# A two-layer block in emulated fp32 on one core: the feed-forwards' first products for 16 of 22 column pairs by Strassen's seven products

## The chip, the core and the metric

The kernel runs on one core of one Trainium2 chip. A core has five engines with instruction queues of their own: TensorE (PE) multiplies matrices and writes to PSUM; VectorE (DVE), ScalarE (ACT) and GpSimd (POOL) work on tiles in SBUF and, except POOL here, read PSUM; SyncE (SP) issues the loads. Each engine runs its queue in order and waits at an instruction until what it needs is there. The metric is the device time of one execution in microseconds (us); the time of a kernel is the median of its runs.

## The reference

The input is x of 512 tokens by 1024 features, and two blocks are applied to it, with four gated feed-forwards among their parts:

```python
def swiglu_ffn(x, w_in, w_out):
    gate, up = jnp.split(x @ w_in, 2, axis=-1)
    return (jax.nn.silu(gate) * up) @ w_out

# first block
x = x + 0.5 * rms_norm(swiglu_ffn(rms_norm(x, norm_pre[l, 0]), ffn1_w_in[l], ffn1_w_out[l]), norm_post[l, 0])
x = x + rms_norm(token_mixer(rms_norm(x, norm_pre[l, 1]), ...), norm_post[l, 1])
x = x + 0.5 * rms_norm(swiglu_ffn(rms_norm(x, norm_pre[l, 2]), ffn2_w_in[l], ffn2_w_out[l]), norm_post[l, 2])
# second block
h = h + 0.5 * swiglu(rms_norm_2(h, ffn1_norm[i]), ffn1_w_in[i], ffn1_w_out[i])
h = h + merged @ w_out[i]                      # two kinds of attention and a gate
h = h + 0.5 * swiglu(rms_norm_2(h, ffn2_norm[i]), ffn2_w_in[i], ffn2_w_out[i])
h = h + sigmoid(rms_norm_2(h, ple_norm[i]) @ w_ple_gate[i]) * (p[i] @ w_ple_proj[i])
```

`w_in` is 1024 x 5632 (2816 gate columns, then 2816 up columns), `w_out` 2816 x 1024, everything in fp32. The change concerns `x @ w_in` of the four feed-forwards, which the kernel calls f1 and f2 (first block), f3 and f4 (second block).

## The kernel before

Activations lie with features on the partitions: x is 8 tiles of 128 features by 512 tokens. An fp32 product is emulated: each operand is split into a high part in TensorE's fast fp32 format and the low rest, and `mm3` (L258 to L261) sums three matmuls, high x high, high x low and low x high. A weight block goes through `wpiece` (L243 to L248): SP loads 128 columns of 8 k-tiles (a raw tile of 128 x 1024, three buffers), ScalarE writes the high part (L247), VectorE subtracts it from the raw tile and writes the low part (L248). Activations are split in the same way (`split`, L309 to L311). `lin` (L274 on) makes one output tile: 8 k-tiles times three matmuls of 512 columns into one PSUM bank.

In `ffn` the norm is applied late. The parts `us` hold x times the norm's gain; the sum of squares (ScalarE squares, POOL adds, L376) gives a factor for each token, which TensorE spreads over the partitions (L357) and VectorE copies to R (L395). Of the 22 pairs m, each 128 gate columns and the same 128 up columns, `lin` makes two banks; VectorE multiplies both by R on the way out of PSUM (L465, L466), ScalarE applies Silu, VectorE multiplies the two (L468), and the result is split at once into hi and lo (L310, L311), the operands of the second product. For f1, f2 and f3 `lin_ahead` computes pairs 0 and 1 in halves of 256 tokens while the phase before finishes; f4 has no such start. `late_constants`, rows that later phases need, is called at m = 2 of f1. `out_post` makes the second product (tiles f1o0, f1o1, ...: 22 k-tiles each, in three weight pieces) and the last of its tiles in halves of 256 tokens; then it applies the second norm and prepares the input of the next phase.

The order of the instructions is the work of a scheduler that goes by the program's order, the priorities from it and buffers that come free; parts of the mixers have a table of their own. So instructions of neighbouring pairs stand interleaved on an engine: in the trace TensorE runs a pair's 48 matmuls without a gap while VectorE splits weights two pairs ahead.

## Time and profile before

| | |
|---|---|
| runs | 2243.27, 2245.18, 2248.12 us; median 2245.18 |
| profiled execution | 2246.1 us, of which the span of the trace is 2244.3 |
| busy share of TensorE, VectorE, ScalarE, GpSimd | 99%, 51%, 39%, 6% |
| matmuls | 10922 |
| first products of f1, f2, f3, f4 (stretches of the span) | 219.98, 219.55, 219.10, 240.70 us |

The span is the time from the first to the last instruction in the trace. Busy shares are means over the span; matmuls overlap, so TensorE's share does not say how near to its peak it is. A tile's name in a row leaves out numbers: `f_12h_h` is the high part of activation 12 of a feed-forward, `f1o_p` an output bank of f1's second product. In brackets behind a row stands the idle time before it and what ended it.

### The profile page before, as it was taken

Reading aid. Unit: us, or ns where it says so; the run is one execution under the profiler, and the core shown is the slowest. Engines: PE = TensorE matmul, PEld = TensorE weight load, DVE = VectorE, ACT = ScalarE, POOL = GpSimd, SP = SyncE. Lnnn points to the kernel's source line nnn. Section 1 sums busy time; section 2 is a strip of 40 time slices with the busy share of each in tenths; the row PEclk is TensorE's granted clock in tenths of the full one; section 3 lists DMA queues with packets and bytes.
Section 4 is the critical chain, followed back from the end, with each engine's and each line's share of the span. In section 5 each row is a group of like instructions: output and inputs, shape, how many; then the busy total and the mean of one; then the engine's idle time right before and its main releaser. Section 6 shows DMA issues by size and latency. Waiting matters only on the chain.

```text
span 2244.3 us, 27350 instructions
## 1 busy us (share of the span) xinstructions
PE 2218.9 (99%) x10922; PEld 1844.9 (82%) x10922; DVE 1151.8 (51%) x1913; ACT 881.6 (39%) x1348; POOL 126.3 (6%) x168
## 2 busy tenths in 40 slices
PE   8999999999999999999999999999999999999999
PEld 7888888888788888889888888887877788888887
DVE  5644423878647544324644432487754554444334
ACT  4323323556545323223433222477654443323222
POOL 4000001100112000001000000000000010000000
PEclk9999999999989999999999999999999999999999
...
GB/s 152 94 96 102 88 100 94 85 66 77 38 47 85 94 102 96 90 100 83 97 100 94 92 96 101 97 75 51 63 80 29 84 108 99 94 95 96 97 108 66
DMA packets 364835, 197.20 MB, mean 88 GB/s; under 512 B 10007, under 2 KB 356516, under 8 KB 364708
## 3 DMA queue, kind: packets, MB, share of 16 engines
...
q14 instruction: 41, 0.34, 0.0%
q0 software_dynamic: 608, 0.09, 0.0%
...
## 4 chain that ended last, share of the span: by engine, by line
PE 97%; DVE 1%; ACT 1%; DMA 0%; issue 0%; SPq 0%; DVEq 0%; ACTq 0%
PE f1o_p L259 2%; PE f2o_p L260 2%; PE f1o_p L260 2%; PE f2o_p L259 2%; PE f2o_p L261 2%; PE f1o_p L261 2%; PE f4o_p L260 2%; PE f4o_p L259 2%; PE f3o_p L259 2%; PE f3o_p L260 2%; PE f3o_p L261 2%; PE f4o_p L261 2%; PE gt_p L259 1%; PE gt_p L260 1%; PE gt_p L261 1%; PE f_p L260 1%
## 5 line engine op out<-in xcount | busy, mean ns | idle before, releaser
L248 DVE TENSOR_TENSOR f1o_l<-f1o_r,f1o_h 128x1024 fp32r<-128x1024 f32 (+1 forms) x24 | 27.3, 1136 | 76.6 <-ACT f1o_h L247 76.6
L248 DVE TENSOR_TENSOR f2o_l<-f2o_r,f2o_h 128x1024 fp32r<-128x1024 f32 (+1 forms) x24 | 27.3, 1136 | 76.6 <-ACT f2o_h L247 76.6
L247 ACT ACTIVATE f1o_h<-f1o_r 128x1024 fp32r<-128x1024 f32 (+1 forms) x24 | 23.8, 990 | 85.7 <-PE f1o_p L260 73.0
L247 ACT ACTIVATE f2o_h<-f2o_r 128x1024 fp32r<-128x1024 f32 (+1 forms) x24 | 23.8, 990 | 85.7 <-PE f2o_p L260 73.0
L247 ACT ACTIVATE f4o_h<-f4o_r 128x1024 fp32r<-128x1024 f32 (+1 forms) x24 | 23.8, 990 | 85.3 <-PE f4o_p L260 53.2
L247 ACT ACTIVATE f3o_h<-f3o_r 128x1024 fp32r<-128x1024 f32 (+1 forms) x24 | 23.8, 990 | 85.3 <-PE f3o_p L260 53.2
L248 DVE TENSOR_TENSOR f3o_l<-f3o_r,f3o_h 128x1024 fp32r<-128x1024 f32 (+1 forms) x24 | 27.2, 1135 | 54.0 <-ACT f3o_h L247 54.0
L248 DVE TENSOR_TENSOR f4o_l<-f4o_r,f4o_h 128x1024 fp32r<-128x1024 f32 (+1 forms) x24 | 27.2, 1135 | 52.9 <-ACT f4o_h L247 52.9
L84 ACT ACT_TABLE_LOAD x36 | 46.2, 1283 | 1.4 <-PEq L1348 0.8
L376 POOL TENSOR_TENSOR f_acc<-f_acc,f_sq 128x256 f32<-128x256 f32 (+1 forms) x42 | 39.0, 929 | 127.5 <-ACT f_sq L375 110.0
L376 POOL TENSOR_TENSOR m_acc<-m_acc,m_sq 128x256 f32<-128x256 f32 (+1 forms) x18 | 20.0, 1114 | 349.0 <-ACT m_sq L375 349.0
L376 POOL TENSOR_TENSOR pl_acc<-pl_acc,pl_sq 128x512 f32<-128x512 f32 x6 | 10.3, 1710 | 340.7 <-ACT pl_sq L375 340.7
L261 PE MATMUL m1o_p<-mix_h,m1o_l 128*128 128x256 f32 (+1 forms) x88 | 29.4, 336 | 0.0
L260 PE MATMUL m1o_p<-mix_l,m1o_h 128*128 128x256 f32 (+1 forms) x88 | 29.4, 336 | 0.0
L259 PE MATMUL m1o_p<-mix_h,m1o_h 128*128 128x256 f32 (+1 forms) x88 | 28.7, 337 | 0.0
L376 POOL TENSOR_TENSOR f2p_acc<-f2p_acc,f2p_sq 128x512 f32<-128x512 f32 x6 | 7.7, 1287 | 323.2 <-ACT f2p_sq L375 323.2
L376 POOL TENSOR_TENSOR f1p_acc<-f1p_acc,f1p_sq 128x512 f32<-128x512 f32 x6 | 7.7, 1288 | 321.5 <-ACT f1p_sq L375 321.5
L259 PE MATMUL wo_p<-mg_h,wo_h 128*128 128x512 f32 x64 | 24.7, 389 | 0.0
L260 PE MATMUL wo_p<-mg_l,wo_h 128*128 128x512 f32 x64 | 24.7, 389 | 0.0
L261 PE MATMUL wo_p<-mg_h,wo_l 128*128 128x512 f32 x64 | 24.7, 389 | 0.0
L94 ACT ACTIVATE l<-l 128x384 f32<-128x384 f32 (+1 forms) x48 | 24.0, 558 | 0.7 <-DVE l L951 0.6
L247 ACT ACTIVATE pg_h<-pg_r 128x1024 fp32r<-128x1024 f32 x8 | 8.5, 1061 | 39.9 <-PE pg L498 12.7
...
## 6 DMA issues: line engine op xcount, KB each, us to landing
...
```

Of the source, the lines that this page charges most:

```text
L84: ld = S.preload_act_table_set(name).ins
L94: i = S.activation(out, in_, func, **kw).ins
L247: S.activation(hi, raw, AF.Copy)
L248: V.tensor_tensor(lo, raw, hi.bitcast(F32), ALU.subtract)
L259: M.matmul(o, w[0], u[0], start=first, stop=False)
L260: M.matmul(o, w[0], u[1], start=False, stop=False)
L261: issued["last"] = M.matmul(o, w[1], u[0], start=False, stop=last).ins.name
L376: G.tensor_tensor(acc[:, sl], acc[:, sl], q[:, sl], ALU.add)
```

## The change

Pairs 6 to 21 of each feed-forward are computed by Strassen's scheme in Winograd's form. The 1024 features fall into two halves of four k-tiles, the 512 tokens into two halves of 256, and gate and up columns are the two halves of the third dimension. Seven products of four k-tiles and 256 tokens (named by their input forms b11, b21, n1, t3, t2, b22, t4) replace eight. Pairs 0 to 5 stay as they were (`direct`).

- `strassen_input`: VectorE writes the normalised input un = x * gain * R (8 times 128 x 512); sums and differences of its quarters are made in place, and 28 forms of 128 x 256 are split into high and low parts (ScalarE and VectorE, 28 operations each).
- `strassen_pair`: two raw tiles r0 (gate) and r1 (up); POOL makes four sums of 128 x 512 from them, in place, as the weights' forms b, c, d beside a = r0; 3 x 1024 and 1 x 512 columns of high and low parts. The products go into two banks ab and cd; ScalarE copies halves of ab (sab), VectorE makes the outputs o1 (gate) and o2 (up) in five operations of 256 columns, then Silu and the product. No multiplication by R is left in these pairs.
- `mm3` only passes on a flag, since a bank now has several open sums.
- In `ffn` all 22 splits of the results stand after the last pair in the program; `late_constants` comes after them. Raw tiles get four buffers instead of three, the activation pool 70 instead of 72. The first Strassen pair's sums are placed behind the norm's last addition (`nx.summed`). One more row of constants (`norm_post`) is loaded at the start.

```diff
--- before.py
+++ after.py
@@ -27,6 +27,9 @@
+NDIRECT = 6
+HT = T // 2
+HK = KD // 2
@@ -52,8 +55,8 @@
-    act = ctx.enter_context(tc.tile_pool(name="act", bufs=72))
-    wraw = ctx.enter_context(tc.tile_pool(name="wraw", bufs=3))
+    act = ctx.enter_context(tc.tile_pool(name="act", bufs=70))
+    wraw = ctx.enter_context(tc.tile_pool(name="wraw", bufs=4))
@@ -175,10 +178,8 @@
-        load_rows(["norm_post", "ffn1_norm_2", "mix_norm_2", "ffn2_norm_2", "ple_norm_2", "hgrn_norm", "mlstm_norm",
+        load_rows(["ffn1_norm_2", "mix_norm_2", "ffn2_norm_2", "ple_norm_2", "hgrn_norm", "mlstm_norm",
-        for i, j in ((0, 0), (1, 2)):
-            V.tensor_scalar(gph[:, i * KD:(i + 1) * KD], cols("norm_post", j * KD, KD), 0.5, None, ALU.mult)
@@ -389,7 +390,7 @@
-            V.tensor_tensor(acc, acc, q, ALU.add)
+            self.summed = V.tensor_tensor(acc, acc, q, ALU.add).ins.name
@@ -449,24 +450,154 @@
         return nx
 
 
+    def strassen_input(x, nx, R, forms, between):
+        un = [None] * KD
+        def normed(k):
+            un[k] = A(f"{nx.name}_n{k}")
+            V.scalar_tensor_tensor(un[k], x[k], nx.g(k), R, ALU.mult, ALU.mult)
+        def form(k, name, src, sign=1.0):
+            t = A(f"{nx.name}_{name}{k}", F32R)
+            hi, lo = t[:, 0:HT], t[:, HT:]
+            S.activation(hi, src, AF.Copy, scale=sign)
+            if sign > 0:
+                V.tensor_tensor(lo, src, hi.bitcast(F32), ALU.subtract)
+            else:
+                V.scalar_tensor_tensor(lo, src, sign, hi.bitcast(F32), ALU.mult, ALU.subtract)
+            forms[k][name] = hi, lo
+        between(0)
+        for k in range(KD):
+            normed(k)
+            form(k % HK, "b21" if k >= HK else "b11", un[k][:, 0:HT])
+        between(1)
+        for k in range(HK):
+            d, b12, b22 = un[k], un[k][:, HT:], un[HK + k][:, HT:]
+            V.tensor_tensor(d[:, 0:HT], b12, d[:, 0:HT], ALU.subtract)
+            V.tensor_tensor(d[:, HT:], b22, b12, ALU.subtract)
+            form(k, "n1", d[:, 0:HT], -1.0)
+            form(k, "t3", d[:, HT:])
+        between(2)
+        for k in range(HK):
+            d, b21, b22 = un[k], un[HK + k][:, 0:HT], un[HK + k][:, HT:]
+            V.tensor_tensor(d[:, 0:HT], b22, d[:, 0:HT], ALU.subtract)
+            V.tensor_tensor(b21, d[:, 0:HT], b21, ALU.subtract)
+            form(k, "t2", d[:, 0:HT], -1.0)
+        between(3)
+        for k in range(HK):
+            form(k, "b22", un[HK + k][:, HT:])
+            form(k, "t4", un[HK + k][:, 0:HT])
+    def strassen_pair(w, c0, c1, forms, name, done, behind=None):
+        r0, r1 = (wraw.tile([P, KD, P], F32, tag="raw", name=f"{name}_r{i}") for i in range(2))
+        for r, c in ((r0, c0), (r1, c1)):
+            nc.sync.dma_start(out=r, in_=w[:, c:c + P].rearrange("(k p) c -> p k c", p=P))
+        def parts(r, nm, n=KD):
+            if n == KD:
+                hi, lo = whi.tile([P, n, P], F32R, tag="hi", name=nm + "_h"), wlo.tile([P, n, P], F32R, tag="lo",
+                                                                                     name=nm + "_l")
+            else:
+                hi, lo = (act.tile([P, n, P], F32R, tag="a", name=f"{nm}_{j}") for j in "hl")
+            S.activation(hi, r, AF.Copy)
+            V.tensor_tensor(lo, r, hi.bitcast(F32), ALU.subtract)
+            return [(hi[:, k, :], lo[:, k, :]) for k in range(n)]
+        first, last = slice(0, HK), slice(HK, KD)
+        s1 = act.tile([P, HK, P], F32, tag="a", name=name + "_s1")
+        in_turn(behind, G.tensor_tensor(s1, r1[:, first], r1[:, last], ALU.add))
+        G.tensor_tensor(r1[:, first], r0[:, first], r1[:, first], ALU.add)
+        g1 = parts(r0, name + "a")
+        G.tensor_tensor(r0[:, first], r0[:, first], s1, ALU.add)
+        G.tensor_tensor(r0[:, last], r0[:, last], r0[:, first], ALU.add)
+        yield
+        g2, g3, g4 = parts(s1, name + "b", HK), parts(r1, name + "c"), parts(r0, name + "d")
+        def product(o, ws, form, start, stop, more=False):
+            for k in range(HK):
+                mm3(o, ws[k], forms[k][form], start and k == 0, stop and k == HK - 1, more)
+        ab, cd = ps(name + "_ab"), ps(name + "_cd")
+        (a, b), (c, d) = ((t[:, 0:HT], t[:, HT:]) for t in (ab, cd))
+        sab, o1, o2 = A(name + "_s"), A(name + "_o1"), A(name + "_o2")
+        product(a, g1[:HK], "b11", True, False)
+        product(b, g1[HK:], "b21", False, True)
+        yield
+        S.activation(sab[:, HT:], b, AF.Copy)
+        V.tensor_tensor(o1[:, 0:HT], a, sab[:, HT:], ALU.add)
+        product(c, g2, "n1", True, False)
+        product(d, g3[:HK], "t3", False, True)
+        product(a, g4[:HK], "t2", False, True, True)
+        S.activation(sab[:, 0:HT], a, AF.Copy)
+        V.tensor_tensor(o2[:, HT:], c, sab[:, 0:HT], ALU.add)
+        V.scalar_tensor_tensor(o2[:, HT:], o2[:, HT:], -1.0, d, ALU.mult, ALU.subtract)
+        yield
+        product(c, g4[HK:], "b22", False, False, True)
+        product(d, g3[HK:], "t4", False, True, True)
+        V.tensor_tensor(o1[:, HT:], c, sab[:, 0:HT], ALU.add)
+        V.scalar_tensor_tensor(o2[:, 0:HT], d, -1.0, sab[:, 0:HT], ALU.mult, ALU.subtract)
+        done(o1, o2)
+        yield
     def ffn(x, nx, w_in, w_out, post, nxt, ahead, name):
         if banks["nm"] != NF:
             psum_pools(m=NF, x=8 - NF)
         us, R, _ = nx.factor()
         table("silu_and_others")
-        hs = []
-        for m in range(KF):
-            if m == 2 and name == "f1":
-                late_constants()
+        hs = [None] * KF
+        def direct(m):
             n = f"{name}_{m}"
-            pg = lin(w_in, m * P, us, n + "g")
-            pu = lin(w_in, DFF + m * P, us, n + "u")
-            gr, ur = A(n + "gr"), A(n + "ur")
+            return lin(w_in, m * P, us, n + "g"), lin(w_in, DFF + m * P, us, n + "u")
+        def gated(m, gr, ur):
+            lut(gr, gr, AF.Silu)
+            V.tensor_tensor(ur, gr, ur, ALU.mult)
+            hs[m] = ur
+        def evict(m, pg, pu):
+            gr, ur = A(f"{name}_{m}gr"), A(f"{name}_{m}ur")
             V.tensor_tensor(gr, pg, R, ALU.mult)
             V.tensor_tensor(ur, pu, R, ALU.mult)
-            lut(gr, gr, AF.Silu)
-            V.tensor_tensor(ur, gr, ur, ALU.mult)
-            hs.append(split(ur, n + "h"))
+            gated(m, gr, ur)
+        forms = [{} for _ in range(HK)]
+        pairs = {m: strassen_pair(w_in, m * P, DFF + m * P, forms, f"{name}_{m}",
+                                  lambda gr, ur, m=m: gated(m, gr, ur), nx.summed if m == NDIRECT else None)
+                 for m in range(NDIRECT, KF)}
+        ready = {m: direct(m) for m in range(3)}
+        run(pairs[NDIRECT], 1)
+        def between(i):
+            for m in ((0, 1), (2,), (3,), ())[i]:
+                evict(m, *ready.pop(m))
+            if i < 3:
+                ready[3 + i] = direct(3 + i)
+        strassen_input(x, nx, R, forms, between)
+        for m in range(4, NDIRECT):
+            evict(m, *(ready.pop(m) if m in ready else direct(m)))
+        run(pairs[NDIRECT], 1)
+        for m in range(NDIRECT, KF):
+            run(pairs[m], 1)
+            if m + 1 < KF:
+                run(pairs[m + 1], 2)
+            run(pairs[m])
+        hs = [split(hs[m], f"{name}_{m}h") for m in range(KF)]
+        if name == "f1":
+            late_constants()
         table("sqrt_and_others")
         if post is not None:
             return out_post(x, w_out, hs, post, 1, nxt, ahead, name)
@@ -1299,7 +1430,9 @@
-    load_rows(["norm_pre"], "a", nc.sync)
+    load_rows(["norm_pre", "norm_post"], "a", nc.sync)
+    for i, j in ((0, 0), (1, 2)):
+        V.tensor_scalar(gph[:, i * KD:(i + 1) * KD], cols("norm_post", j * KD, KD), 0.5, None, ALU.mult)
```

In the changed file lines have moved by one above `ffn` (L247, L248 and L311 are now L248, L249 and L312) and by more in it: evictions L571 and L572, low parts of the pairs' weights L513, sums from PSUM L537, L542, L543, L547 and L548, product L566.

How instructions stand now. First VectorE in the middle of f1. Before, the rows of one pair (`f1_9gr` and `f1_9ur` are the gate and up results, `_l` a low part of weights or of a result):

```order
L465 TENSOR_TENSOR f1_9gr_1224<-f1_9g_p_1168,f1_R_529 128x512 [waits PE_49]
L248 TENSOR_TENSOR f1_11g_0_l_1309<-f1_11g_0_r_1306,f1_11g_0_h_1308 128x1024 [waits DMAHW7_49,Activation_49]
L466 TENSOR_TENSOR f1_9ur_1225<-f1_9u_p_1199,f1_R_529 128x512 [waits PE_49]
L468 TENSOR_TENSOR f1_9ur_1225<-f1_9gr_1224,f1_9ur_1225 128x512 [waits DVE_49,Activation_49]
L248 TENSOR_TENSOR f1_11u_0_l_1340<-f1_11u_0_r_1337,f1_11u_0_h_1339 128x1024 [waits DMAHW0_49,Activation_49]
L311 TENSOR_TENSOR f1_9h_l_1231<-f1_9ur_1225,f1_9h_h_1230 128x512 [waits Activation_49]
```

Now, the rows of one period (`_cd`, `_ab` are the banks, `_s` is sab, `12b_l` the low part of pair 12's form b, and `r0`, `r1` are the raw tiles):

```order
L542 TENSOR_TENSOR f1_11_o2_1556<-f1_11_cd_1553,f1_11_s_1554 128x256 [waits Activation_49]
L543 SCALAR_TENSOR_TENSOR f1_11_o2_1556<-f1_11_o2_1556,f1_11_cd_1553 128x256 [waits DVE_49]
L513 TENSOR_TENSOR f1_12b_l_1664<-f1_12_s1_1654,f1_12b_h_1663 128x512 [waits Activation_49]
L537 TENSOR_TENSOR f1_12_o1_1678<-f1_12_ab_1675,f1_12_s_1677 128x256 [waits Activation_49]
L513 TENSOR_TENSOR f1_12c_l_1668<-f1_12_r1_1651,f1_12c_h_1667 128x1024 [waits DMAHW3_49,Activation_49]
L547 TENSOR_TENSOR f1_11_o1_1555<-f1_11_cd_1553,f1_11_s_1554 128x256 [waits PE_49]
L548 SCALAR_TENSOR_TENSOR f1_11_o2_1556<-f1_11_cd_1553,f1_11_s_1554 128x256
L513 TENSOR_TENSOR f1_12d_l_1672<-f1_12_r0_1650,f1_12d_h_1671 128x1024 [waits Activation_49]
L513 TENSOR_TENSOR f1_13a_l_1781<-f1_13_r0_1773,f1_13a_h_1780 128x1024 [waits DMAHW4_49,Activation_49]
L566 TENSOR_TENSOR f1_11_o2_1556<-f1_11_o1_1555,f1_11_o2_1556 128x512 [waits DVE_49,Activation_49]
```

Six rows have become ten; low parts of pair 12 stand between sums of pair 11, and the low part of pair 13's form a stands ahead of the product of pair 11.

Second TensorE, at the end of f1's first products. Before (`f1_21u_p` is the bank of the last up product, `f1o0_p` the first bank of the second product):

```order
L260 MATMUL f1_21u_p_2063<-f1_u7l_179,f1_21u_0_h_2059 128x512
L261 MATMUL f1_21u_p_2063<-f1_u7h_178,f1_21u_0_l_2060 128x512
L259 MATMUL f1o0_p_2119<-f1_0h_h_543,f1o0_0_h_2103 128x512 [waits Activation_49]
L260 MATMUL f1o0_p_2119<-f1_0h_l_544,f1o0_0_h_2103 128x512
L261 MATMUL f1o0_p_2119<-f1_0h_h_543,f1o0_0_l_2104 128x512 [waits DVE_49]
L259 MATMUL f1o0_p_2119<-f1_1h_h_553,f1o0_0_h_2103 128x512
```

Now (`f1_t23` is form t2 of the fourth k-tile, `f1_b220` form b22 of the first):

```order
L262 MATMUL f1_21_ab_2782<-f1_t23_914,f1_21d_l_2779 128x256
L260 MATMUL f1o0_p_3115<-f1_0h_h_2908,f1o0_0_h_3099 128x512 [waits Activation_49]
L261 MATMUL f1o0_p_3115<-f1_0h_l_2909,f1o0_0_h_3099 128x512 [waits DVE_49]
L262 MATMUL f1o0_p_3115<-f1_0h_h_2908,f1o0_0_l_3100 128x512
L260 MATMUL f1o0_p_3115<-f1_1h_h_2912,f1o0_0_h_3099 128x512 [waits Activation_49]
L261 MATMUL f1o0_p_3115<-f1_1h_l_2913,f1o0_0_h_3099 128x512 [waits DVE_49]
L262 MATMUL f1o0_p_3115<-f1_1h_h_2912,f1o0_0_l_3100 128x512
L260 MATMUL f1o0_p_3115<-f1_2h_h_2916,f1o0_0_h_3099 128x512 [waits Activation_49]
L260 MATMUL f1_21_cd_2783<-f1_b220_917,f1_21d_h_2778 128x256 [waits DVE_49]
L261 MATMUL f1_21_cd_2783<-f1_b220_917,f1_21d_h_2778 128x256
L262 MATMUL f1_21_cd_2783<-f1_b220_917,f1_21d_l_2779 128x256
```

The second product's first seven matmuls have come between the last two pieces of pair 21, and where the first activation had no wait for VectorE they now wait for ScalarE and VectorE in turn.

Third VectorE, after the direct pairs of f1. Before, from pair 4's product on (`7u_0_l` is a low part of weights, `5gr` and `5ur` are evictions):

```order
L468 TENSOR_TENSOR f1_4ur_865<-f1_4gr_864,f1_4ur_865 128x512 [waits DVE_49,Activation_49]
L248 TENSOR_TENSOR f1_7u_0_l_1052<-f1_7u_0_r_1049,f1_7u_0_h_1051 128x1024 [waits DMAHW0_49,PE_49,Activation_49]
L311 TENSOR_TENSOR f1_4h_l_871<-f1_4ur_865,f1_4h_h_870 128x512 [waits Activation_49]
L465 TENSOR_TENSOR f1_5gr_936<-f1_5g_p_880,f1_R_529 128x512
L466 TENSOR_TENSOR f1_5ur_937<-f1_5u_p_911,f1_R_529 128x512
L468 TENSOR_TENSOR f1_5ur_937<-f1_5gr_936,f1_5ur_937 128x512 [waits DVE_49,Activation_49]
```

Now, around the same evictions (`f1_t43` is form t4 of the fourth k-tile; `f1_7a_l` and `f1_6b_l` are low parts of weights):

```order
L473 TENSOR_TENSOR f1_t42_932<-f1_n6_719,f1_t42_932 128x256 [waits Activation_49]
L473 TENSOR_TENSOR f1_b223_935<-f1_n7_724,f1_b223_935 128x256 [waits Activation_49]
L473 TENSOR_TENSOR f1_t43_938<-f1_n7_724,f1_t43_938 128x256 [waits Activation_49]
L572 TENSOR_TENSOR f1_5ur_948<-f1_5u_p_872,f1_R_532 128x512 [waits PE_49]
L513 TENSOR_TENSOR f1_7a_l_1043<-f1_7_r0_1035,f1_7a_h_1042 128x1024 [waits DMAHW0_49,Activation_49]
L513 TENSOR_TENSOR f1_6b_l_954<-f1_6_s1_606,f1_6b_h_953 128x512 [waits Activation_49]
L566 TENSOR_TENSOR f1_4ur_942<-f1_4gr_941,f1_4ur_942 128x512 [waits DVE_49,Activation_49]
L537 TENSOR_TENSOR f1_6_o1_968<-f1_6_ab_965,f1_6_s_967 128x256 [waits Activation_49]
```

The low part of pair 7's form a stands behind the last of the input's forms and the evictions of the direct pairs 4 and 5, ahead of pair 6's form b.

## Rows read from the trace of the kernel before

**Rows 1.** Page: busy time of the engines; chain that ended last, by engine

```profile
PE 2218.9 (99%) x10922; PEld 1844.9 (82%) x10922; DVE 1151.8 (51%) x1913; ACT 881.6 (39%) x1348; POOL 126.3 (6%) x168
...
PE 97%; DVE 1%; ACT 1%; DMA 0%; issue 0%; SPq 0%; DVEq 0%; ACTq 0%
```

**Rows 2.** Windows (span, length, busy, clock, DMA): the four stretches, first and sum

```profile
41.85:261.83 219.98, 218.60 (x968) 180.72 (x968) 113.40 (x176) 71.34 (x89) 0.00 (x0) 1.00 0.35 102
...
sum 899.33, PE 897.95 PEld 742.80 DVE 442.00 ACT 290.98 POOL 0.00; mean PE 224.49 PEld 185.70 DVE 110.50 ACT 72.74 POOL 0.00
```

**Rows 3.** Timeline of TensorE (start, duration, line, output<-inputs): matmuls of 512 columns

```profile
299.90 0.39 PE L259 MATMUL f1o_p<-f_12h_h,f1o_h 128*128 128x512 f32 x1
...
320.98 0.39 PE L259 MATMUL f1o_p<-f_21h_h,f1o_h 128*128 128x512 f32 x1
```

**Rows 4.** Timeline of TensorE: matmuls of 256 columns, first and last of 66

```profile
366.54 0.28 PE L259 MATMUL f1o_p<-f_0h_h,f1o_h 128*128 128x256 f32 x1
...
374.33 0.28 PE L261 MATMUL f1o_p<-f_21h_h,f1o_l 128*128 128x256 f32 x1
```

**Rows 5.** Windows (busy PE, PEld, DVE, ACT, POOL, then PEclk): three behind the second products

```profile
381.50:387.37 5.87, 4.69 (x38) 4.42 (x38) 5.23 (x12) 4.15 (x10) 0.51 (x1) 1.00 0.74 188
387.37:390.78 3.41, 3.41 (x18) 3.41 (x18) 3.41 (x9) 1.78 (x5) 1.55 (x3) 0.50 0.51 137
393.36:410.71 17.35, 17.35 (x147) 17.30 (x144) 15.52 (x31) 8.67 (x21) 6.18 (x8) 1.00 0.01 2
```

**Rows 6.** Timeline of VectorE, shapes alone; source L376 (min/median/max ns) of POOL

```profile
41.18 1.23 DVE L248 TENSOR_TENSOR f_2g_l<-f_2g_r,f_2g_h 128x1024 fp32r<-128x1024 f32 x1 [5.29 <-ACT f_2g_h L247]
42.32 1.22 DVE L248 TENSOR_TENSOR f_2u_l<-f_2u_r,f_2u_h 128x1024 fp32r<-128x1024 f32 x1
...
52.23 0.69 DVE L465 TENSOR_TENSOR f_0gr<-f_p,f_R 128x512 f32<-128x512 f32 x1
52.84 0.68 DVE L466 TENSOR_TENSOR f_0ur<-f_p,f_R 128x512 f32<-128x512 f32 x1
...
393.21 0.43 DVE L442 TENSOR_TENSOR x<-x,f_y 128x256 f32<-128x256 f32 x1
393.55 0.97 DVE L314 SCALAR_TENSOR_TENSOR m_u5l<-x,pcola,m_u5h 128x256 fp32r<-128x256 f32 x1
...
396.22 0.48 DVE L314 SCALAR_TENSOR_TENSOR m_u7l<-x,pcola,m_u7h 128x256 fp32r<-128x256 f32 x1 [0.18 <-ACT m_u7h L313]
...
L376 POOL TENSOR_TENSOR f1p_acc<-f1p_acc,f1p_sq x6: 1285/1286/1292, 293.9 to 368.8; 128x512 f32<-128x512 f32 x6
```

**Rows 7.** Timeline of ScalarE: the first feed-forward's end

```profile
261.84 1.06 ACT L247 ACTIVATE f1o_h<-f1o_r 128x1024 fp32r<-128x1024 f32 x1 [2.60 <-issue]
...
263.54 0.64 ACT L310 ACTIVATE f_21h_h<-f_21ur 128x512 fp32r<-128x512 f32 x1 [0.64 <-DVE f_21ur L468]
```

**Rows 8.** Timeline of VectorE and GpSimd beside each other, two places

```profile
1061.74 0.41 DVE L441 TENSOR_TENSOR f_y<-f_y,f2p 128x256 f32<-128x256 f32 x1
...
1061.93 0.74 POOL L376 TENSOR_TENSOR f_acc<-f_acc,f_sq 128x256 f32<-128x256 f32 x1 [0.40 <-ACT f_sq L375]
...
1062.18 0.77 DVE L442 TENSOR_TENSOR x<-x,f_y 128x256 f32<-128x256 f32 x1
...
1344.66 0.75 DVE L314 SCALAR_TENSOR_TENSOR m_u2l<-x,pcolb,m_u2h 128x512 fp32r<-128x512 f32 x1
...
1344.76 1.79 POOL L376 TENSOR_TENSOR m_acc<-m_acc,m_sq 128x512 f32<-128x512 f32 x1 [13.17 <-ACT m_sq L375]
```

**Rows 9.** Timelines and waits of TensorE (41 to 262): the first feed-forward's start

```profile
41.85 0.47 PE L259 MATMUL f_2g_p<-f_u0h,f_2g_h 128*128 128x512 f32 x1
...
47.56 1.23 DVE L248 TENSOR_TENSOR f_3u_l<-f_3u_r,f_3u_h 128x1024 fp32r<-128x1024 f32 x1 [2.14 <-ACT f_3u_h L247]
...
50.14 0.60 PE L357 MATMUL f_sp<-ident,f_y 128*128 128x128 f32 x4
...
PE f_5g_p L259 <- DVE f_2gr L465: 1.4, 1, 1.4
```

More of the change, by code (lines that the diff above doesn't have):

```diff
@@ L256, in wcols, with mm3 @@
         return r
-    def mm3(o, w, u, first, last):
-        M.matmul(o, w[0], u[0], start=first, stop=False)
-        M.matmul(o, w[0], u[1], start=False, stop=False)
-        issued["last"] = M.matmul(o, w[1], u[0], start=False, stop=last).ins.name
+    def mm3(o, w, u, first, last, more=False):
+        M.matmul(o, w[0], u[0], start=first, stop=False, skip_group_check=more)
+        M.matmul(o, w[0], u[1], start=False, stop=False, skip_group_check=more)
+        issued["last"] = M.matmul(o, w[1], u[0], start=False, stop=last, skip_group_check=more).ins.name
     issued = {}
```

## The prediction

> **What bounds the kernel now.** I read the page first: TensorE (PE) is busy for 99% of the span and the chain that ended last runs on it for 97% [rows 1]. So only two things can move the time: TensorE's own work, and holes that open in it. Then I looked by windows at the stretches in which the four feed-forwards compute their first products: 899.33 us in all, TensorE busy for 897.95 of them, VectorE (DVE) for half, GpSimd (POOL) never [rows 2]. Next I took TensorE's pace from its timeline, by starts, since matmuls overlap and their durations do not add. With 512 columns 93 steps from 299.90 to 320.98 take 21.08 us: 226.7 ns each [rows 3]. With 256 columns, each matmul with weights of its own as the changed kernel has them, 65 steps from 366.54 to 374.33 take 7.79 us: 119.8 ns [rows 4]; over a longer stretch 147 of them fill 17.35 us, 118 ns, beside a busy DVE and POOL [rows 5]. Half the columns cost 53% of the time, not 50%.
>
> The Trainium skill's page "TensorE: Matmul & The Clock Gate", section "Back-to-back issue gap", gives columns / 2.4 GHz + 2.5 ns for the isolated gap, 215.8 and 109.2 ns here. The trace shows 226.7 and 119.8, so that page would make the saving below 1.19 us for a pair where the rows give 0.80. I go by the rows.
>
> **TensorE's work.** A pair (128 columns of gate and the same of up) had 2 x 8 x 3 = 48 matmuls of 512 columns: 48 x 226.7 = 10.88 us. Seven products of four k-tiles and half the tokens are 7 x 4 x 3 = 84 matmuls of 256 columns: 84 x 119.8 = 10.06, say 10.08 us. That is 0.80 us less, for 64 pairs (16 in each of four feed-forwards) **-51.2 us**. The arithmetic falls by an eighth, the time by 7.4%. With 118 ns [rows 5] it would be 62 us; this is the lower end.
>
> **A pair in the steady state.** What has to stay hidden under 10.08 us. DVE, by durations [rows 6]: three 1024-wide low parts (1.23), one of 512 and one product (0.69 each), three 256-wide sums (0.43) and two with a scalar (0.48) = 7.3 us; by starts (1.14, 0.61, 0.34, and 0.40 for those with a scalar, taking off the same 0.08) 6.5 us. ScalarE (ACT): 3 x 1.06 for the high parts and four operations of at most 0.64 [rows 7] = 5.7 us. POOL: four adds of 1.285 [rows 6] = 5.1 us. Each has room. What the sum does not show is that POOL and DVE can hold each other up: a DVE sum with both inputs in SBUF, 0.43 us alone [rows 6], took 0.77 beside a POOL add, and a POOL add of 512 took 1.79 instead of 1.285 beside a DVE operation of the same kind; a DVE operation with one input in PSUM kept its 0.41 while POOL started beside it [rows 8]. This is told, as a rule against the change, by "GPSIMD Engine Reference", section "Specifications", of the Trainium skill: the two share their SBUF interfaces, with contention where DVE has two SBUF inputs; these rows agree. In a pair the DVE operations with both inputs in SBUF are 3 x 1.23 + 2 x 0.69 = 5.1 us, and POOL's adds 5.1: 10.2 if they exclude each other for their whole durations. But rows 8 show less: the 512 pair together ran from 1344.66 to 1346.55, 1.89 us for 0.75 + 1.285 = 2.03, so each meeting gives 0.14 back, and the gap between durations and steps is not exclusive either. With four to eight meetings and 5 x 0.08 I get 8.7 to 9.3 us, under 10.08, by 0.8 to 1.4.
>
> Whether single waits open is a matter of deadlines, counted from the first matmul of product n1. The order on DVE is fixed (shown above). The first sum of o2 waits for t2 (4.32) and the ACT copy behind it, and is through with its partner at 5.7, before b22 needs the bank at 7.2. o1's first half waits for the next pair's b11 and b21 (7.2), is done at 8.2, the next c's low part at 9.3; o2's second half waits for t4 (10.08) until 10.55; then the next d's low part is done 1.6 us into the next period, needed at 2.88 + 0.24 = 3.1, and the low part of a behind it at 2.8, needed at 4.56. A POOL add in the way costs 1.285 - 0.14 = 1.1 us: d at 2.7, a at 3.9, both still 0.4 to 0.7 early. So **0** for the steady pairs; two adds in the way of d would be 0.7 late. Bounds: 0 to +1.5 us for a pair (rival A).
>
> **The start of a feed-forward.** Before, TensorE went from the norm's sums straight on, at 41.85 in the first one [rows 9]. Now DVE has to normalise the input and make 28 forms and 16 differences while the direct products run. In the first three, two direct pairs were computed ahead; eight products remain, 8 x 24 x 226.7 ns = 43.5 us, then b11 and b21 of pair 6 (2.88), and after two matmuls more the b11 of pair 7 stands in the order, which needs 7a's low part: 41.85 + 43.5 + 2.88 + norm matmuls of some 0.8 = about 89.1 us. DVE gets the transposed norm factor at 50.14 + 0.5 [rows 9], copies it and evicts four banks (5 x 0.61) until 53.7. From there to 7a's low part the order counts 7 of 1024, 8 of 512 with a scalar (0.66 by the same deduction), 12 of 512, 36 of 256 and 8 of 256 with a scalar: 7.98 + 5.28 + 7.32 + 12.1 + 3.2 = 35.9 us, so 89.6. That is 0.5 us late with no wait at all, and POOL's adds for pair 7 run just before: one or two meetings of 1.1. I take 2.0 us for each of the first three, **+6.0**. Lower bound 0; upper: by durations instead of steps the work is 6 us longer, so 6 each (18). Waits on loads, as DVE's 2.14 us at 47.56 [rows 9], lie earlier than the factor and cost nothing more. The fourth has no products ahead: 12 x 5.44 = 65 us of cover, 0.
>
> The first Strassen pair has no neighbour to interleave at its end: t2 is followed at once by b22 into the bank that ACT and DVE have to read first (copy 0.4, sum 0.43, sum with scalar 0.48, and semaphores: about 1.5 us). Four times: **+6.0** (2 to 12).
>
> **The end of a feed-forward.** Before, the next phase's weights and all but the last two activations were split when TensorE reached them; the last split ran at 263.54 [rows 7], 1.7 us behind the first use of its neighbours, far ahead of its own. Now all 22 splits come after the last pair in the order, and f1o0's first matmul waits for the first of them, which stands on ACT behind the copy that waits for t2 of pair 21. From t2's end T: copy T+0.6, high part T+1.2, low part T+1.9, o2's second sum T+2.9. In T to T+6.1 TensorE has 7 matmuls of 512 and 24 of 256, 7 x 0.227 + 2.88 = 4.5: 1.6 us lost, four times: **+6.4** (3 to 12). Behind it a split every 0.64 us [rows 7] feeds three matmuls of 0.68, and weight parts stand between; the last is ready at about T+19, needed at about T+24. That keeps ahead; if it did not, this is another us or two, within the bound.
>
> **Small.** One more row load on the queue ahead of the first weights: +0.4. The 1.4 us wait of f_5g behind late constants [rows 9] goes, since these now stand behind the first feed-forward's products: -1.4. Nothing else moves outside the feed-forwards; the loads per pair are the same bytes.
>
> **Sum.** -51.2 + 6.0 + 6.0 + 6.4 + 0.4 - 1.4 = -33.8 us. The profiled execution took 2246.1 (span 2244.3 and 1.8 around it): 2212.3. It stands 0.9 above the runs' median, so 2211.4; I say 2212.
>
> **Rivals.**
> A, slower: the shared SBUF interface becomes the bound. For it: the 10.2 us above, without what meetings give back, lie over 10.08, and no row shows both engines loaded like this for long. If all four adds stop DVE for 1.1 us each and POOL makes no use of DVE's waits for PSUM, a period is 7.3 + 4 x 1.1 = 11.7 us against 10.88 before: +0.8 x 64 = +51, with starts and ends of 17 about 2314. It decides from a period of 10.08 + 33.8 / 64 = 10.6 us on. Against it: operations on PSUM were not held up, and they leave POOL 2.2 us and DVE's idle 3 us in each period.
> B, a smaller gain: deadlines are missed by 0.1 to 0.2 us a pair (+6 to +13), the starts take 5 instead of 2 (+9), and holes make the clock fall: 0.50 was granted (1.2 of 2.4 GHz) for 3.41 us after a stretch in which TensorE was busy for 4.69 of 5.87 us [rows 5], 1.7 us lost for each. 2224 to 2242. For it: three new holes in each feed-forward; against: the 1.4 us hole of f_5g [rows 9] left the clock at 1.00 in that window [rows 2].
> C, a larger gain: holes at starts and ends are covered by half or more, or the pace is 118 ns: 2192 to 2203. For it: the 118 of rows 5.
> D, the page's isolated gap holds in such long streams: 64 x 1.19 = 76 saved, 2246 - 76 + 17 = 2187. Against it stand both paces in rows 3 and 4.
> E, no change: A's mechanism at a period of 10.6.
>
> **Chances.** Forecast (2203 to 2224) 0.62, A 0.08, B 0.16, C 0.09, D 0.02, E 0.03. Likeliest time 2212, its own range 2203 to 2224. To leave out no more than 2 in 10, the range takes in most of B and a part of C: 2200 to 2240. A measurement of this kernel can tell 0.2%, 4.5 us, from no change: faster 0.89, same 0.03, slower 0.08.
>
> **What would show it.** Right: steady pairs 10.0 to 10.2 us apart on TensorE, its matmul starts 119 to 121 ns apart; in each feed-forward three holes of 1 to 3 us (before pair 7's b11, before pair 6's b22, before f1o0) and hardly any between; 1024-wide low parts on DVE at 1.2 to 2.0 us beside POOL. Wrong: holes before t2 or b11 in every pair (A, B), a granted clock of 0.50 behind the holes (B), a pace under 117 ns (C, D), or splits that make TensorE wait far into f1o0.

## The result: 1.5% faster, near the predicted time, with four terms of the sum off

Four runs of the changed kernel took 2210.55 to 2216.97 us, median 2212.62, against a median of 2244.22 in four runs before: the ratio is 0.985, with a 95% interval of 0.9831 to 0.9869. A second comparison gave 0.9866 (0.9847 to 0.9885). The forecast was 2212 us, in a range of 2200 to 2240. The profiled execution took 2210.55 (span 2208.8), 35.5 us less than the one before.

The changed kernel's page and windows (the first feed-forward's stretch and the sum of the four, as in [rows 1, 2]):

```profile
PE 2169.6 (98%) x13226; PEld 1910.9 (87%) x13226; DVE 1451.9 (66%) x2441; ACT 1043.2 (47%) x1716; POOL 519.2 (24%) x423
...
PE 90%; DVE 8%; ACT 1%; issue 0%; DMA 0%; SPq 0%; DVEq 0%; ACTq 0%
```

```profile
43.42:249.33 205.91, 203.18 (x1519) 194.96 (x1518) 167.69 (x243) 98.83 (x158) 94.98 (x62) 1.00 0.36 103
...
sum 846.54, PE 835.58 PEld 798.48 DVE 675.18 ACT 400.00 POOL 382.97; mean PE 208.89 PEld 199.62 DVE 168.79 ACT 100.00 POOL 95.74
```

TensorE still sets the time, but the chain now steps to VectorE for 8% of the span, and the stretches have 11 us without a matmul where they had 1.4. The stretches end before b22 and t4 of pair 21, which stand in the second product. Counted to that product's last matmul, the four feed-forwards take 10.4, 8.7, 8.5 and 9.4 us less, 36.9 together. The start of the program, from the first matmul to the first feed-forward's first product, takes 1.9 us more, and all the rest 0.5 less.

The pace, from the same pair product eight pairs apart in TensorE's timeline (start, duration):

```profile
132.98 0.28 PE L260 MATMUL f_cd<-f_n,f_10b_h 128*128 128x256 f32 x1
...
213.62 0.28 PE L260 MATMUL f_cd<-f_n,f_18b_h 128*128 128x256 f32 x1
```

80.64 us for eight periods: 10.08 each, as forecast. Every period from pair 7 on, in all four feed-forwards, is 10.08 us. The holes are at the three places named, in TensorE's waits (total, times, longest) and timeline:

```profile
PE f_cd L260 <- DVE f_o L543: 5.6, 4, 1.4
...
PE pcola L153 <- DMA prowa<-in_norm_post_dram: 2.8, 1, 2.8
...
PE f_ab L262 <- DVE f_7a_l L513: 1.5, 3, 0.7
...
PE f1o_p L260 <- ACT f_0h_h L311: 1.0, 1, 1.0
```

```profile
98.11 0.28 PE L262 MATMUL f_ab<-f_t,f_6d_l 128*128 128x256 f32 x1
99.77 0.38 PE L260 MATMUL f_cd<-f_b,f_6d_h 128*128 128x256 f32 x1 [1.39 <-DVE f_o L543]
...
248.06 0.28 PE L262 MATMUL f_ab<-f_t,f_21d_l 128*128 128x256 f32 x1
249.33 0.50 PE L260 MATMUL f1o_p<-f_0h_h,f1o_h 128*128 128x512 f32 x1 [0.99 <-ACT f_0h_h L311]
250.06 0.50 PE L261 MATMUL f1o_p<-f_0h_l,f1o_h 128*128 128x512 f32 x1 [0.23 <-DVE f_0h_l L312]
```

From start to start, less the matmul's own pace, and with the 0.1 us by which the first matmul behind a wait is slower, the first pair's hole is 1.65 us and the end's 1.15 + 0.6 = 1.76.

| term | forecast | measured |
|---|---|---|
| 64 pairs | -51.2 | -51.2 |
| start, pair 7's a, three times | +6.0 | +2.2 |
| first pair, t2 to b22, four times | +6.0 | +6.6 |
| end, first splits, four times | +6.4 | +7.0 |
| program's start | +0.4 | +1.9 |
| late constants' wait | -1.4 | -1.4 |
| sum | -33.8 | -34.9 (spans: -35.5) |

The +1.9 at the program's start is that of this execution. The stretch takes 39.8 us here and 38.9 to 39.8 in the ten profiled executions that leave the start's code as it is, against 37.9 in the one profiled execution before: +1.0 to +1.9.

### The profile page after: what moved, and what is told of

Same layout as the page of the kernel before. It is cut to its first block, busy times and chain, and to the rows that moved or that the text cites. A ratio compares the mean times of both kernels' runs of the same rounds, so it can differ in the third digit from the quotient of the medians.

```text
span 2208.8 us, 33325 instructions
## 1 busy us (share of the span) xinstructions
PE 2169.6 (98%) x13226; PEld 1910.9 (87%) x13226; DVE 1451.9 (66%) x2441; ACT 1043.2 (47%) x1716; POOL 519.2 (24%) x423
## 4 chain that ended last, share of the span: by engine, by line
PE 90%; DVE 8%; ACT 1%; issue 0%; DMA 0%; SPq 0%; DVEq 0%; ACTq 0%
PE f_cd L260 6%; PE f_cd L262 6%; PE f_cd L261 6%; PE f_ab L262 4%; PE f_ab L261 4%; PE f_ab L260 4%; PE f3o_p L261 2%; PE f1o_p L261 2%; PE f4o_p L261 2%; PE f2o_p L261 2%; PE f4o_p L262 2%; PE f3o_p L262 2%; PE f3o_p L260 2%; PE f4o_p L260 2%; PE f2o_p L260 2%; PE f1o_p L260 2%
## 5 line engine op out<-in xcount | busy, mean ns | idle before, releaser
L521 POOL TENSOR_TENSOR f_r<-f_r,f_s 128x512 f32<-128x512 f32 x64 | 101.8, 1591 | 257.3 <-DVE f_8a_l L513 34.1
L518 POOL TENSOR_TENSOR f_s<-f_r 128x512 f32<-128x512 f32 x64 | 102.2, 1598 | 173.0 <-DMA f_r<-in_ffn_w_in_dram 71.4
L541 ACT ACTIVATE f_s<-f_ab 128x256 f32<-128x256 f32 x64 | 24.5, 383 | 219.3 <-PE f_ab L262 219.3
L519 POOL TENSOR_TENSOR f_r<-f_r,f_r 128x512 f32<-128x512 f32 x64 | 103.5, 1618 | 5.0
L522 POOL TENSOR_TENSOR f_r<-f_r 128x512 f32<-128x512 f32 x64 | 84.2, 1315 | 5.0
L542 DVE TENSOR_TENSOR f_o<-f_cd,f_s 128x256 f32<-128x256 f32 x64 | 27.2, 424 | 74.1 <-ACT f_s L541 74.1
L536 ACT ACTIVATE f_s<-f_ab 128x256 f32<-128x256 f32 x64 | 24.5, 383 | 100.2 <-PE f_ab L262 100.2
L249 DVE TENSOR_TENSOR f2o_l<-f2o_r,f2o_h 128x1024 fp32r<-128x1024 f32 (+1 forms) x24 | 27.2, 1134 | 66.5 <-ACT f2o_h L248 66.5
L377 POOL TENSOR_TENSOR f_acc<-f_acc,f_sq 128x256 f32<-128x256 f32 (+1 forms) x42 | 39.6, 944 | 128.0 <-ACT f_sq L376 127.3
L249 DVE TENSOR_TENSOR f1o_l<-f1o_r,f1o_h 128x1024 fp32r<-128x1024 f32 (+1 forms) x24 | 27.2, 1135 | 56.7 <-ACT f1o_h L248 56.6
L249 DVE TENSOR_TENSOR f3o_l<-f3o_r,f3o_h 128x1024 fp32r<-128x1024 f32 (+1 forms) x24 | 27.2, 1135 | 43.1 <-ACT f3o_h L248 43.1
L249 DVE TENSOR_TENSOR f4o_l<-f4o_r,f4o_h 128x1024 fp32r<-128x1024 f32 (+1 forms) x24 | 27.2, 1135 | 43.1 <-ACT f4o_h L248 43.1
L248 ACT ACTIVATE f2o_h<-f2o_r 128x1024 fp32r<-128x1024 f32 (+1 forms) x24 | 23.7, 987 | 64.2 <-PE f2o_p L261 64.2
L248 ACT ACTIVATE f3o_h<-f3o_r 128x1024 fp32r<-128x1024 f32 (+1 forms) x24 | 23.7, 988 | 63.9 <-PE f3o_p L261 45.0
L248 ACT ACTIVATE f4o_h<-f4o_r 128x1024 fp32r<-128x1024 f32 (+1 forms) x24 | 23.7, 988 | 63.9 <-PE f4o_p L261 45.0
L248 ACT ACTIVATE f1o_h<-f1o_r 128x1024 fp32r<-128x1024 f32 (+1 forms) x24 | 23.7, 989 | 62.3 <-PE f1o_p L261 52.6
L97 ACT ACTIVATE f_o<-f_o 128x512 f32<-128x512 f32 x64 | 40.4, 632 | 23.7 <-DVE f_o L547 21.1
L537 DVE TENSOR_TENSOR f_o<-f_ab,f_s 128x256 f32<-128x256 f32 x64 | 27.1, 423 | 34.0 <-ACT f_s L536 33.6
L566 DVE TENSOR_TENSOR f_o<-f_o,f_o 128x512 f32<-128x512 f32 x64 | 43.4, 679 | 0.0
```

Of the source, the lines that this page charges most:

```text
L248: S.activation(hi, raw, AF.Copy)
L249: V.tensor_tensor(lo, raw, hi.bitcast(F32), ALU.subtract)
L377: G.tensor_tensor(acc[:, sl], acc[:, sl], q[:, sl], ALU.add)
L518: in_turn(behind, G.tensor_tensor(s1, r1[:, first], r1[:, last], ALU.add))
L519: G.tensor_tensor(r1[:, first], r0[:, first], r1[:, first], ALU.add)
L521: G.tensor_tensor(r0[:, first], r0[:, first], s1, ALU.add)
```

## Experiments

Each run's time is compared by stretches. Single times differ by several us through the mixers, where a granted clock of 0.50 lasts longer in one execution than in another, at places that no experiment touched; and all kernels but the last two ran once. "Feed-forwards" is the sum over the four, from the first product to the second product's last matmul, against the changed kernel. Each edit is to the changed kernel.

**Are the steady pairs bound by TensorE, and how near is the rest?** First the kernel without POOL's adds, which computes other sums:

```diff
-        in_turn(behind, G.tensor_tensor(s1, r1[:, first], r1[:, last], ALU.add))
-        G.tensor_tensor(r1[:, first], r0[:, first], r1[:, first], ALU.add)
...
-        G.tensor_tensor(r0[:, first], r0[:, first], s1, ALU.add)
-        G.tensor_tensor(r0[:, last], r0[:, last], r0[:, first], ALU.add)
...
-        g2, g3, g4 = parts(s1, name + "b", HK), parts(r1, name + "c"), parts(r0, name + "d")
+        g2, g3, g4 = parts(r1[:, last], name + "b", HK), parts(r1, name + "c"), parts(r0, name + "d")
```

> Leaves out GpSimd's four adds in each Strassen pair: the weights' forms b, c and d are taken from raw columns, so 64 pairs compute other sums with the same work on every other engine. Theory (the steady pair is bound by TensorE, and what VectorE and GpSimd take from each other is hidden): the period stays 10.08 us; low parts of 1024 on VectorE go from a mean of 1.39 back to 1.22 us and come about 0.5 us earlier before their use; only the holes ahead of pair 7's b11 (0.6 to 0.95 us in three feed-forwards) close, so the profiled time falls by 1 to 4 us, to about 2208. Rival (VectorE and GpSimd together set the pace of the pairs): the period falls by 0.3 us or more, 20 us in all.

The period stayed 10.08 us, and low parts of 1024 were back at 1.22 us. The feed-forwards took 3.8 us less, because the holes shrank: those ahead of pair 7's b11 from 2.2 to 1.05 us in all, and, which was not expected, each first pair's from 1.65 to 1.25 and each end's by 0.3; the order on TensorE had changed there with the edit. The run took 2202.25 us; the rest of the difference is in the mixers and at the start. Then two adds more:

```diff
+        for i in range(2):
+            xs = act.tile([P, HK, P], F32, tag="a", name=f"{name}_x{i}")
+            G.tensor_tensor(xs, r1[:, first], r1[:, last], ALU.add)
```

> Adds two more GpSimd sums of 128x512 into scratch behind the second add of each Strassen pair; nothing else. GpSimd then works 6.1 + 2.6 to 3.2 = about 9 us in a period of 10.08, VectorE as before. Theory (deadlines: the new adds fall beside the low parts of d and a, each can hold VectorE up by about 1 us, and these are only 0.5 to 1.0 us early): d and a come late by 0.3 to 1 us in every pair, the period becomes 10.4 to 11.1, the time 2230 to 2275. Rival (only the sum of work counts: both engines still have room in 10.08 us, VectorE being idle for over 2 us of it): period 10.08, time within 5 us of 2211.

The run took 2332.86 us, feed-forwards +116: the period is 11.95 us, where 10.4 to 11.1 were expected, and from pair 8 on every t2 waits for d's low part. POOL (the added pair is the row of x2), VectorE and TensorE of that kernel at pair 14:

```profile
190.80 2.99 POOL L522 TENSOR_TENSOR f_x<-f_r 128x512 f32<-128x512 f32 x2
...
192.57 2.30 DVE L513 TENSOR_TENSOR f_14d_l<-f_r,f_14d_h 128x1024 fp32r<-128x1024 f32 x1
...
194.92 0.39 PE L262 MATMUL f_ab<-f_t,f_14d_l 128*128 128x256 f32 x1 [1.42 <-DVE f_14d_l L513]
```

A low part of 1024 that takes 1.22 us alone takes 2.30 here. POOL worked 47 of 60 us and VectorE 53, so by sums of work there was room, and that rival is out. Counted from the trace over 110 us, a POOL add or a VectorE operation with both inputs in SBUF runs for 98% of the time here, for 94% in the changed kernel, and for 50% without adds. The prediction's sum for the steady pair, with six adds, comes near too: 5.1 us of such VectorE operations and 6 x 1.285 of POOL's are 12.8; less 0.14 for each of four to eight meetings, 11.7 to 12.3, and less the 5 x 0.08 that the prediction also took off, 11.3 to 11.9. My size was too small, since I had charged only the two deadlines. That the two engines' operations as a whole set the period, and not the place of the new adds in POOL's queue, is argued from the 98% and was not tested by itself.

**Is the gain 0.80 us a pair?**

```diff
-NDIRECT = 6
+NDIRECT = 14
```

> Strassen for pairs 14 to 21 only (8 of 22 in each feed-forward), all else as in the changed kernel. Theory (each Strassen pair saves 48 x 226.7 - 84 x 120 ns = 0.80 us and the holes are a fixed price for each feed-forward): 32 pairs fewer cost 25.6 us; the holes ahead of the second pair's b11 (2.2 us in all) close since VectorE has eight pairs more of cover; first pair's and end's holes stay. In the feed-forwards' stretches together +23 to +26 us, time about 2234. Rival (part of the gain comes from elsewhere, as fewer evictions or the wait behind late constants): the loss is clearly under 20 us.

Feed-forwards +23.2 us. There is no hole ahead of the second pair's b11, and 1.65 us stand at each first pair and 1.76 at each end as before, which makes 25.6 - 2.2 = 23.4. So with 8 pairs and with 16 the gain goes with their number. (The run took 2241.21 us, with 8 us more in the first mixer, where the clock was at 0.50 for longer.)

**What bounds the start?** With `NDIRECT = 5` alone:

> Strassen from pair 5 on (17 of 22). Theory (at a feed-forward's start VectorE's chain of input forms is the bound, and the direct products only cover it): TensorE saves 4 x 0.8 = 3.2 us, but loses a cover of 10.88 us while VectorE's chain falls by only 2 x 1.14 + 3 x 0.61 = 4.1 us, so the hole ahead of the second pair's b11 grows from 0.6 to about 7 us in each feed-forward: 20 to 28 us slower, 2230 to 2239. Rival (VectorE's low parts and forms only follow a scheduler's order and find room): 2 to 3 us faster, 2208.

The run took 2247.35 us, feed-forwards +33.9, but it says nothing on the start: `between` still called `direct` for pair 5, so this pair was computed both ways (a feed-forward has no matmul of 512 columns fewer, and 84 more of 256). That is four times 10.08 us more, less 6.4 us of holes that closed. With `NDIRECT = 5` and this line as well, pair 5 is computed once:

```diff
-            if i < 3:
+            if 3 + i < NDIRECT:
```

> Strassen from pair 5 on (17 of 22), and pair 5 computed in that way only (the earlier run with this limit also computed it directly). Theory (VectorE's chain of input forms bounds a feed-forward's start): TensorE's work falls by 3.2 us, its cover by 10.88 us and VectorE's chain by about 4.1, so holes of 5 to 7.5 us more open at the first Strassen pairs of each feed-forward: 17 to 27 us slower over the feed-forwards than the changed kernel. Rival (the chain finds room): 3 us faster.

The run took 2228.97 us, feed-forwards +16.2: +4.9, +4.7, +7.3 and, in the fourth with two more direct pairs of cover, -0.75. The chain of input forms is the bound in the first three, and not in the fourth, which I had counted in; so the sum is just under the range. The wait stands ahead of n1 and is for ScalarE's high part of b, behind the forms in its queue, not for VectorE's part of a. Some of ScalarE's forms wait in turn for VectorE's differences, so the chain is one of both engines:

```profile
PE f_cd L260 <- ACT f_5b_h L512: 16.3, 3, 7.0
```

The third hole is the longest, and there VectorE lost 1.8 us beside POOL's first two sums for pair 6: these took 1.30 and 1.36 us, and two of VectorE's forms 1.14 and 1.51 instead of 0.42. In the first two feed-forwards VectorE's forms kept 0.42, and the first of these sums took 12.96 and 13.13 us:

```profile
73.20 12.96 POOL L518 TENSOR_TENSOR f_s<-f_r 128x512 f32<-128x512 f32 x1 [24.47 <-PE f_4u_p L262]
...
1105.99 1.36 POOL L519 TENSOR_TENSOR f_r<-f_r,f_r 128x512 f32<-128x512 f32 x1
...
1106.12 1.51 DVE L473 TENSOR_TENSOR f_t<-f_n,f_t 128x256 fp32r<-128x256 f32 x1
```

With these holes, of 4.7 to 7.1 us, the clock fell, as in the third feed-forward (windows; granted clock behind the busy times):

```profile
1114.90:1121.70 6.80, 3.93 (x18) 3.94 (x19) 6.80 (x19) 3.71 (x10) 6.72 (x2) 0.50 0.00 0
```

**The first pair.** Pair 7's first matmul behind pair 6's t2:

```diff
-        product(a, g1[:HK], "b11", True, False)
+        prev = issued["last"] if turn else None
+        product(a, g1[:HK], "b11", True, False, prev=prev)
...
-                                  lambda gr, ur, m=m: gated(m, gr, ur), nx.summed if m == NDIRECT else None)
+                                  lambda gr, ur, m=m: gated(m, gr, ur), nx.summed if m == NDIRECT else None, m == NDIRECT + 1)
```

> Makes pair 7's first matmul stand behind pair 6's t2, as in every later pair (before, it stood behind the first two matmuls of pair 6's n1). Theory (the hole of 1.55 us between t2 and b22 of pair 6 comes from this order alone): the hole closes in four feed-forwards, 6.2 us less; but n1 of pair 6 now has nothing in front while its low part of b stands behind 7a's on VectorE, so a hole of 1 to 1.7 us opens there where 0.5 to 0.95 stood in three of them: 2 to 4 us less in all, about 2207. Rival (the bank is read late because VectorE is behind at the start, whatever TensorE's order): the hole stays or moves, no gain.

(`mm3` puts the first matmul behind `prev`.) Feed-forwards -3.6 us: there is no hole at b22, and one of 1.3 to 1.75 us at n1 (0.37 in the fourth), where TensorE waits for b's low part:

```profile
PE f_cd L262 <- DVE f_6b_l L513: 4.3, 4, 1.6
```

So the hole at b22 came from TensorE's order. The run took 2213.0 us all the same, for 5.7 us more in the first mixer, where the clock was at 0.50 for 27 us instead of 14. Then form b's parts of pair 6 were made early as well:

```diff
         g1 = parts(r0, name + "a")
+        g2 = parts(s1, name + "b", HK) if behind is not None else None
...
+        g2 = g2 or parts(s1, name + "b", HK)
```

> As the run on the first pair's order, and besides the high and low parts of form b of pair 6 are made with those of a, ahead of the input's forms. Theory (what was left there was n1 waiting for b's low part behind 7a's on VectorE): no hole of over 0.3 us at the first pair in any feed-forward; 1.65 x 4 + 0.5 to 0.95 in three = 8.5 to 9 us less than in the changed kernel over the feed-forwards' stretches, if the longer chain of forms does not come late itself. Rival (VectorE's chain of forms is then late at n1 or t3 by its 0.6 us more): 3 to 6 us less.

The run took 2206.43 us, feed-forwards -7.6, with no hole over 0.25 us at the first pair in any of them. The last 1 us of the 8.5 to 9 expected is in such small ones.

**The end.** Three splits earlier:

```diff
+        early = (14, 16, 18)
...
-        hs = [split(hs[m], f"{name}_{m}h") for m in range(KF)]
+            if m in early:
+                i = early.index(m)
+                hs[i] = split(hs[i], f"{name}_{i}h")
+        hs = [h if isinstance(h, tuple) else split(h, f"{name}_{m}h") for m, h in enumerate(hs)]
```

> The splits of activations 0, 1 and 2 are placed behind pairs 14, 16 and 18 instead of after pair 21; all other splits stay at the end. Theory (the hole of 1.15 + 0.6 us ahead of each second product is the wait for these splits alone, which stand behind the copy of the last pair's sum): the hole closes in all four feed-forwards, and the matmuls on ready activations cover the last pair's own chain: 5 to 7 us less, about 2204. Rival (in a period whose low parts are only 0.5 us early there is no room for a split of 0.61 us on VectorE and 0.64 on ScalarE): three periods in each feed-forward grow by 0.1 to 0.6 us, and the gain falls under 3 us.

The run took 2206.07 us, feed-forwards -6.4: the hole is gone, and all periods stay 10.08.

**The program's start.** norm_post's rows as a group of their own:

```diff
-    load_rows(["norm_pre", "norm_post"], "a", nc.sync)
+    load_rows(["norm_pre"], "a", nc.sync)
...
     run(lin_ahead(I["ffn1_w_in"][0], FIRST, ws, nx.us, "f1"))
+    load_rows(["norm_post"], "c", nc.gpsimd)
...
```

> Loads norm_post's rows as a group of their own after the direct products begun ahead, by GpSimd's queue, instead of with norm_pre on the queue of the first weights. Theory (the first transpose of rows waits 2.8 us for this load, and the first products with it): the stretch from the first matmul to f1's first product falls by 1 to 1.9 us from 39.8. Rival (the cause is the fourth raw tile, by which another weight load of 512 KB stands ahead of x's second half on the queue): it stays within 0.4 us of 39.8.

The stretch took 40.3 us: no gain, though the trace had named that load with 2.8 us (1.5 to 2.3 in other executions). It is no clean test, since x's last tiles were issued 0.8 us later as well. SP's loads show another difference, in the changed kernel and then before (start, time on the queue, count):

```profile
4.41 6.23 SPq L245 DMA_DIRECT2D f_r<-in_ffn_w_in_dram  x3
10.68 3.42 SPq L123 DMA_DIRECT2D xt<-in_x_dram  x4
```

```profile
7.76 3.90 SPq L120 DMA_DIRECT2D xt<-in_x_dram  x4
11.78 0.38 SPq L244 DMA_DIRECT2D f_r<-in_ffn_w_in_dram  x1
```

With a fourth raw tile the third of these weight loads no longer waits for a buffer, and x's last tiles are issued 2.9 us later. With them put ahead of the fourth weight:

```diff
-    ws += [wcols(I["ffn1_w_in"][0], KD, c, f"f1_{c}") for c in FIRST[1:]]
+    ws += [wcols(I["ffn1_w_in"][0], KD, c, f"f1_{c}") for c in FIRST[1:3]]
     load_x((2, 3), 0)
     load_x((2, 3), 1)
+    ws += [wcols(I["ffn1_w_in"][0], KD, c, f"f1_{c}") for c in FIRST[3:]]
```

> The changed kernel with the loads of x's last four tiles put ahead of the fourth weight load at the start of the program, as they stood in the kernel before; norm_post's rows stay where the change put them. Theory (moving the rows gave nothing, so the fourth raw tile, by which 512 KB more stand ahead of x's second half, makes the later start): the first 512-column product starts 1 to 1.9 us earlier than 43.4, near 41.9 as before. Rival (the rows' wait of 2.8 us is a cost of its own): 42.9 or later.

The run took 2212.97 us. The first product starts at 42.50, between what the theory and the rival had named. In this kernel, and then in the changed kernel run again on the same chip (first product):

```profile
8.27 3.95 SPq L123 DMA_DIRECT2D xt<-in_x_dram  x4
...
42.50 0.47 PE L260 MATMUL f_2g_p<-f_u0h,f_2g_h 128*128 128x512 f32 x1
```

```profile
42.84 0.47 PE L260 MATMUL f_2g_p<-f_u0h,f_2g_h 128*128 128x512 f32 x1
```

The stretch from the first matmul is 38.8 us, and 38.6 in the combination below, where the same code of the start without this edit gave 38.9 to 39.8. Against the 39.1 and 39.6 of two of these on the same chip, the order of the loads is worth 0.3 to 1.0 us, which two executions with it hardly show clear of the scatter. The rest of the 1.0 to 1.9 us stays open.

**All that helped together** (early splits, pair 7 behind t2 with b early, x's tiles ahead of the fourth weight), and the changed kernel beside it:

> The parts that helped together: the splits of activations 0 to 2 behind pairs 14, 16 and 18; pair 7's first matmul behind pair 6's t2 with b's parts of pair 6 made early; and x's last tiles loaded ahead of the fourth weight. Theory (the holes are separate places on TensorE, so their gains add): 6.4 + 7.6 us over the feed-forwards and 1 to 1.9 at the start, 15 to 16 us less than the changed kernel: about 2197. Rival (closing one hole shifts the lateness to the next place): 8 to 11 us less.

> The changed kernel again, on the same chip as the combination: 2210 to 2214 us.

The medians are 2199.21 and 2216.53 us on one chip, against 2247.72 before: ratios 0.9784 (0.9767 to 0.9802) and 0.9866 (0.9847 to 0.9885). The repeat's median lies above the range given for it. The feed-forwards take 13.8 us less where 6.4 + 7.6 = 14.0 were to be had, so these gains add, though two of the 56 periods were longer (10.66 and 10.31 us). The start is 0.6 us shorter than in the repeat. This version beats both.

## Why the prediction was right

- **TensorE's work** (-51.2): shown, by the period of 10.08 us in 56 neighbouring pairs and by the run with half the pairs. The pace of 119.8 ns from before held through 16 pairs, at 120, so rival D and rival C's faster pace are out. The Trainium skill's page "TensorE: Matmul & The Clock Gate", section "Back-to-back issue gap", gives 109.2 ns for the isolated gap. The trace does not agree for this stream. The 118 ns on which rival C leaned was misread: three of the 147 matmuls of [rows 5] start before the window. The other 144 run from the first of these starts to the second, 121 ns apart:

```profile
393.36 0.36 PE L259 MATMUL m_p<-m_u4h,m_h 128*128 128x256 f32 x1
...
410.71 0.28 PE L261 MATMUL m_p<-m_u7h,m_l 128*128 128x256 f32 x1
```

- **The steady pair** (0): right. In the trace, from pair 8 on, d's low part is ready 0.5 us before its use at the least and 1.0 in the median, and a's 0.18 at the least and 1.06 in the median; 0.4 and 0.7 had been worked out with one POOL add in the way. At its closest in the third feed-forward, VectorE's low parts of c and d meet POOL's second add (of pair 15), and TensorE uses the low part of d right behind:

```profile
1189.63 1.93 DVE L513 TENSOR_TENSOR f_14c_l<-f_r,f_14c_h 128x1024 fp32r<-128x1024 f32 x1 [0.52 <-ACT f_14c_h L512]
...
1190.56 2.17 POOL L519 TENSOR_TENSOR f_r<-f_r,f_r 128x512 f32<-128x512 f32 x1
...
1192.15 1.66 DVE L513 TENSOR_TENSOR f_14d_l<-f_r,f_14d_h 128x1024 fp32r<-128x1024 f32 x1
...
1194.30 0.28 PE L262 MATMUL f_ab<-f_t,f_14d_l 128*128 128x256 f32 x1
```

 Rival A was near: two adds more, and the period grew to 11.95 us. The Trainium skill's page "GPSIMD Engine Reference", section "Specifications", has contention with VectorE where that has two SBUF inputs. The traces agree (2.30 us for 1.22). I had charged 8.7 to 9.3 us of 10.08; the 94% measured are 9.5.
- **The start** (+6.0): too high, at 2.2 us. Being 0.5 us late without contention was nearly the whole of it (0.6 to 0.95 measured). VectorE's chain, from the fourth eviction to pair 7's low part of a, took 35.7 us in the first feed-forward, where 35.9 had been worked out without a meeting. I had added 1.5 us for meetings with POOL. Here POOL paid for most of them: its first add for pair 7 took 4.89 us instead of 1.285 while VectorE's forms kept 0.41, and one form took 0.92 beside the second add:

```profile
82.24 4.89 POOL L518 TENSOR_TENSOR f_s<-f_r 128x512 f32<-128x512 f32 x1 [33.20 <-DVE f_t L475]
87.21 1.46 POOL L519 TENSOR_TENSOR f_r<-f_r,f_r 128x512 f32<-128x512 f32 x1
...
88.04 0.92 DVE L473 TENSOR_TENSOR f_t<-f_n,f_t 128x256 fp32r<-128x256 f32 x1
```

- **First pair and end** (+6.0, +6.4): mechanism and place are shown by closing them. The sizes are 10% low; two thirds of that is the slower first matmul behind each wait, 0.1 us.
- **The program's start** (+0.4): too low, at 1.0 to 1.9. I counted the row load's time on the queue and held that nothing else moves outside the feed-forwards. A fourth raw tile frees a weight load to pass ahead of x, and the prediction gave that no price. It is a part of the cause at most; moving the load that the trace names (norm_post's) gave nothing, and the rest is open.
- **Rival B's clock**: holes of up to 1.76 us left it at 1.00 in all four feed-forwards; those of 4.7 to 7.1 us in the run from pair 5 on did not. Between them, waits of 3.6 us in the run with two adds more were followed by 0.50 in two feed-forwards of three.

The sum's errors, -3.8, +0.6, +0.6 and +0.6 to +1.5, offset each other, and the same kernel's median was 2216.53 us in the repeat. So it is luck that 2212 was met within 1 us; each term was good to about 4 us.
